# Down projection of a decoder layer: 22 plain K tiles replaced by four plain tiles, seven pairs in seven block products, and four plain tiles

## The chip, the cores and the metric

One Trainium2 chip, one of its cores. The metric is the device time of one execution in microseconds (us), the median of several runs. The engines are TensorE (PE, matrix products; its weight loads are shown apart as PEld), VectorE (DVE), ScalarE (ACT), GpSimd (POOL) and SyncE (SP, which only starts transfers here).

## The reference

One decoder layer on 512 tokens of width 1024: a mixer with two attention groups, then a gated channel mixer of width D_FF = 2816. The part that matters here is the last product and what follows it:

```python
h = rms_norm(x, ffn_pre_norm[l])
f = (jax.nn.silu(h @ w_gate[l]) * (h @ w_up[l])) @ w_down[l]
x = x + rms_norm(f, ffn_post_norm[l])
```

`rms_norm` divides a row by the root of its mean square (plus 1e-6) and multiplies by a gain. `w_down` is 2816 x 1024. All data is float32.

## The kernel before

**Precision.** TensorE multiplies in a reduced format (fp32r). Each float32 operand is split in two tiles: `hi` is the operand copied into fp32r by ScalarE, `lo` is the operand minus `hi`, by VectorE. A product is then three matmuls into one PSUM bank: hi by hi, lo by hi, hi by lo.

**Stages.** The input projection, the two attentions, the output projection and its norm, the up and gate products, and the down projection follow each other. The up and gate products already use block products: `ff_seven` (L952) makes two tiles of D_FF at a time with seven products of blocks, whose sums `ff_prep` (L920) builds; a chain `before[0]` (L904) fixes the order of its matmuls. Its results are the 22 tiles `ffr[f]` (128 of D_FF in the partitions, 512 tokens in the columns), which stay in SBUF in the slots of `sslot` (L162, tiles of 128x512).

**The down projection** (L1026 to L1062, the minus lines of the diff). The result is 512 tokens x 1024 columns: four row tiles of 128 tokens by two halves of 512 columns, `acc[i][c]`, eight PSUM banks that are held through the whole stage. The sum over D_FF goes in 22 K tiles of 128. For each, `down_operands(f)` loads 128x1024 of `w_down` (512 KB; `load_w`, L97, on SyncE's queue) into a rotating raw slot, splits it into `whi` and `wlo` (`split_w`, L111 to L115: ScalarE at L104, VectorE at L114) and splits `ffr[f]` into `ffh` (L104) and `ffl` (L1034). `down` (L1037 to L1042) issues three matmuls for one bank, the two halves of the columns and the four rows in turn: 24 matmuls of 128x512 a K tile, 528 in all. No order is fixed by hand: the scheduler may put them as their operands come.

The first 19 tiles (`NF - LAST`) run tile by tile, all eight banks each. The last three (`LAST = 3`) run row by row: for row tile `i` the three tiles' products for its two banks, and then, while TensorE does the next row, its norm: ScalarE sums the squares from PSUM (`row_rsqrt`, L780), VectorE multiplies the banks by the gain `g_ffn` (L1059), a few one-column steps (`rsqrt_mean`, L122 to L134) make the row's factor `rr`/`rs`, VectorE multiplies by it and adds the residual `x2` (L1061), and SyncE writes the half rows (L1062). `big` (L760) gives tiles of 128x1024 out of named rings, `rope_tile` (L190) tiles of 128x2048, `halves` the two halves of the columns, `wide(tag)` two PSUM banks of a ring, `gain(j)` a loaded gain.

## Time and profile before

| what | value |
|---|---|
| median of 3 runs | 688.05 us (687.72 to 688.37) |
| the profiled execution's own time | 687.77 us |
| its span, first to last instruction | 686.0 us |
| mean granted TensorE clock | 0.98 |
| DMA, mean over the span | 128 GB/s, 87.93 MB |
| instructions | 11052 |

The profile is of one execution. It gives the busy time of each engine and its share of the span, the span in 40 slices, the chain of work that ended last (followed back from the last instruction, at each step to what released it), groups of instructions by source line, and the transfers. A row of a group reads: line, engine, operation, output<-inputs (partitions x elements), number, then busy us and mean ns of one, then the idle time of the engine ahead of them and what ended it. `L1040` is line 1040 of the kernel before. A matmul's recorded length is longer than the distance to the next, since matmuls overlap; so the distance from start to start is what counts. The profiled execution lies 1.8 us above its span (start and end that no engine's record covers) and 0.3 us under the median.

### The profile page before, as it was taken

The page shows a single profiled execution, that of the slowest core. Times are in us where ns is not written, and L with a number is a line of the kernel's source. Part 1 is how long each engine was busy: PE and PEld are TensorE (multiplying, and loading weights), DVE is VectorE, ACT ScalarE, POOL GpSimd, SP SyncE. Part 2 cuts the span into 40 slices and gives each one's busy share as a digit, 9 for nine tenths or more (in the row PEclk, how much of TensorE's full clock was granted, in tenths as well). Part 3 has the DMA queues.
Part 4 walks back from the last instruction along what each step waited for, and adds up shares of the span by engine and source line. Part 5 has one row for each costly group of instructions (what it writes and reads, how often), then busy time and mean ns, then how long its engine had stood idle before and what let it go on. Part 6 is the DMA issues. An engine that isn't in the chain of part 4 may idle for free.

```text
span 686.0 us, 11052 instructions
## 1 busy us (share of the span) xinstructions
PE 651.1 (95%) x4141; PEld 583.5 (85%) x4141; DVE 508.7 (74%) x1015; ACT 367.3 (54%) x775; POOL 78.5 (11%) x86
## 2 busy tenths in 40 slices
PE   9999999999899998797889999999999999999995
PEld 5988787999788787675888999999999988888884
DVE  4878897887999978669898898888888477222227
ACT  7443454568799578435564555655565465212213
POOL 0000000111755323315200000000000000000000
PEclk9999999999999999898799999999999999999998
DMA  8446859671121420252313323332323422332203
GB/s 305 153 139 226 277 198 320 235 246 48 47 94 57 159 93 1 93 210 97 108 64 120 111 93 123 96 120 93 123 94 107 167 96 92 102 112 94 93 0 123
DMA packets 27141, 87.93 MB, mean 128 GB/s; under 512 B 3536, under 2 KB 4432, under 8 KB 26192
## 3 DMA queue, kind: packets, MB, share of 16 engines
q1 hardware_dynamic: 27088, 87.23, 37.8%
q8 instruction: 32, 0.52, 0.3%
q14 instruction: 21, 0.17, 0.1%
HBM read 75.16 MB, written 12.06 MB: 127 GB/s over the span
## 4 chain that ended last, share of the span: by engine, by line
PE 75%; DVE 11%; ACT 6%; DMA 4%; issue 2%; SPq 1%; POOL 0%; DVEq 0%; ACTq 0%
PE gw L913 27%; PE acc L1040 16%; PE fm L290 10%; PE gu L893 5%; PE dv L364 3%; PE mixp L684 3%; ACT p L499 2%; PE tr L509 2%; PE vg L386 2%; DMA wraw<-in_wf 2%; PE sc L493 2%; DVE ptl L514 1%; PE sc L494 1%; DVE p L498 1%; PE avn L637 1%
## 5 line engine op out<-in xcount | busy, mean ns | idle before, releaser
L114 DVE TENSOR_TENSOR wlo<-wraw,whi 128x1024 fp32r<-128x1024 f32 (+2 forms) x58 | 69.9, 1208 | 82.2 <-ACT whi L104 82.0
L104 ACT ACTIVATE whi<-wraw 128x1024 fp32r<-128x1024 f32 (+2 forms) x58 | 60.3, 1045 | 111.2 <-PE acc L1040 66.6
L1040 PE MATMUL acc<-whi,ffl 128*128 128x512 f32 x176 | 68.6, 390 | 0.0
L1040 PE MATMUL acc<-wlo,ffh 128*128 128x512 f32 x176 | 68.1, 390 | 0.0
L1040 PE MATMUL acc<-whi,ffh 128*128 128x512 f32 x176 | 67.2, 390 | 0.4 <-ACT ffh L104 0.4
L518 POOL TENSOR_TENSOR p<-p,l 128x384 f32<-128x384 f32 (+3 forms) x60 | 49.2, 848 | 131.2 <-DVE l L548 58.0
L499 ACT ACTIVATE p<-p,nm 128x128 f32<-128x128 f32 (+1 forms) x96 | 53.2, 556 | 15.3 <-DVE nm L498 14.6
L498 DVE CUSTOM_DVE_ANT_0 p<-sc,mask_b 128x128 f32<-128x128 f32 (+1 forms) x96 | 43.9, 483 | 6.7 <-PE sc L494 6.1
L514 DVE TENSOR_TENSOR ptl<-tr,pth 128x384 fp32r<-128x384 f32 (+1 forms) x60 | 35.6, 595 | 5.8 <-ACT pth L513 5.3
L1040 PEld LDWEIGHTS acc<-whi,ffh 128*128 128x128 f32 x176 | 33.0, 188 | 7.4 <-ACT ffh L104 0.6
L513 ACT ACTIVATE pth<-tr 128x384 fp32r<-128x384 f32 (+1 forms) x60 | 30.8, 517 | 15.3 <-PE tr L509 14.9
L1040 PEld LDWEIGHTS acc<-whi,ffl 128*128 128x128 f32 x176 | 33.1, 188 | 6.9
L1040 PEld LDWEIGHTS acc<-wlo,ffh 128*128 128x128 f32 x176 | 33.1, 188 | 6.8
L509 PE MATMUL tr<-ident,p 128*128 128x128 f32 x200 | 34.2, 290 | 3.9 <-DVE rr L127 2.3
L493 PE MATMUL sc<-kst,qst 128*128 128x128 f32 (+2 forms) x96 | 33.5, 357 | 4.5 <-DVE nm L498 2.9
L290 PE MATMUL fm<-xh,whi 128*128 128x512 f32 x128 | 33.5, 396 | 1.5 <-ACT whi L104 1.5
L509 PEld LDWEIGHTS tr<-ident,p 128*128 128x128 f32 x200 | 25.3, 150 | 8.8 <-DVE ptl L514 3.0
L290 PE MATMUL fm<-xh,wlo 128*128 128x512 f32 x128 | 32.6, 391 | 0.0
L290 PE MATMUL fm<-xl,whi 128*128 128x512 f32 x128 | 32.4, 390 | 0.0
L494 PE MATMUL sc<-kst,qst 128*128 128x128 f32 (+2 forms) x96 | 31.0, 326 | 0.0
L290 PEld LDWEIGHTS fm<-xh,whi 128*128 128x128 f32 x128 | 23.6, 188 | 7.3 <-ACT whi L104 2.1
L290 PEld LDWEIGHTS fm<-xl,whi 128*128 128x128 f32 x128 | 24.0, 188 | 5.0
(292 smaller groups left out, 1717.6 us busy)
## 6 DMA issues: line engine op xcount, KB each, us to landing
wraw<-in_wg SPq DMA_DIRECT2D x22, 512.0 KB, 3.4
wraw<-in_wd SPq DMA_DIRECT2D x22, 512.0 KB, 3.3
wu<-in_wu SPq DMA_DIRECT2D x19, 512.0 KB, 3.3
wraw<-in_wf SPq DMA_DIRECT2D x16, 512.0 KB, 4.8
qk<-rope SPq DMA_DIRECT2D x7, 1024.0 KB, 4.8
kst<-qk SPq DMA_DIRECT2D x24, 256.0 KB, 3.8
qst<-qk SPq DMA_DIRECT2D x16, 256.0 KB, 3.1
wraw<-in_wo SPq DMA_DIRECT2D x8, 512.0 KB, 3.5
```

Source lines behind the costliest of these rows:

```text
L104: act.activation(dst, src, AF.Copy)
L114: (lo_eng or dve).tensor_tensor(lo[:, :w], raw[:, :w], f32(hi[:, :w]), OP.subtract)
L290: pe.matmul(pt, w[:, k * P:(k + 1) * P], xx[k], start=(n == 0), stop=(n == 3 * NK - 1))
L493: pe.matmul(sv, lhs, kk[:, 0, :w], start=True, stop=False)
L494: pe.matmul(sv, lhs, kk[:, 1, :w], start=False, stop=True)
L498: dve.tensor_tensor_reduce(pt, sv, mask_b[:, (NT - 1 - i) * P:], -1.0, BIG, OP.add, OP.min, nm)
L499: act.activation(pt, pt, AF.Exp, bias=nm, scale=-1.0, accum_out=l[:, i:i + 1])
L509: pe.transpose(tr[:, n * P:(n + 1) * P], pts[i][:, j * P:(j + 1) * P], ident)
L514: dve.tensor_tensor(ptl[:, sl], trv, f32(pth[:, sl]), OP.subtract)
L518: pool.tensor_tensor(p, p, l.to_broadcast(list(p.shape)), OP.mult)
L913: m = pe.matmul(pt, ww[:, k * P:(k + 1) * P], hx[k], start=(start and n == 0), stop=(n == 11), skip_group_check=True)
L1040: pe.matmul(acc[i][c], a[:, i * P:(i + 1) * P], w[wi][:, c * SEQ:(c + 1) * SEQ], start=(first and n == 0), stop=(last and n == 2))
```

## The change

It rewrites the down projection and leaves the rest (the order of all engines up to the first matmul of the stage is the same, apart from splits of two weight tiles that came early).

*Plain tiles in front.* K tiles 0 to 3 (`PRE`) are plain, 24 matmuls each, by `d_plain`. The four quarters of the result (256 tokens x 512 columns, two banks each) are C11 in `cc`, C12 in `ca`, C21 in `cb`, C22 in `cd`. Then ScalarE copies C12 and C21 to SBUF (`dps`).

*Seven pairs.* Tiles 4 to 17 are taken two at a time. Of a pair, a11 and a12 are the first and second tile's first 256 tokens, a21 and a22 their other 256; b11 and b12 are the first weight tile's two column halves, b21 and b22 the second's. Instead of eight products of blocks, seven are made, in Winograd's form, each of 2 x 3 matmuls of 128x512. They are split in two passes over all seven pairs. The x pass has three (18 matmuls): a11 b11 into `ca`, -(a21+a22)(b11-b12) into `cb`, a12 b21 into `cc`. Then ScalarE copies `ca` and `cb` to SBUF (L1196) and VectorE adds `cc` and `cd` to these copies (L1199, four steps of 128x512). The y pass has the other four (24 matmuls): two more into `ca` and `cb`, and `cd` and `cc` started anew. At its end `ca` and `cd` are taken into the partial results `u2`, `u3`, `p5` (L1211 to L1215), and POOL's queue starts four accumulating transfers (L1218, 256 KB each) that add the saved C12 and C21 onto `u2` and `u3`.

*Plain tiles behind.* Tiles 18 to 21 are plain; of these the last three run row by row as before. Each bank then holds only a part, so VectorE first adds the saved part (L1237, 128x512, eight steps), the squares are read from SBUF, and the gain product (L1239) and the output (L1241, L1242) follow.

*Operands.* `d_load`, `d_sums` and `d_split` make the operands of a step: the sums of blocks and the low parts on VectorE, the high parts on ScalarE (L1044). The order of the two engines' steps and of all matmuls is written by chains (`queued`, `before[0]`). The operands come in the order four plain, x of pairs 0 to 2, y of pair 0, x of 3 to 6, y of 1 to 6, four plain (`YPOS`, `YN`); `ready` holds them two steps ahead of TensorE (more at the start, `PRELEAD`). Split weights lie in the three ring slots of before and in three more inside `hth` and `htl`, which the gate stage no longer needs. The loads of `w_down` for an x step are one tile and a half, for a y step two; the gain's and the residual's loads stand behind them on SyncE's queue.

The diff:

```diff
...
+HOFF, HSLOTS = 8, 3
+PRE, PAIRS = 4, 7
+AHEAD, PRELEAD = 3, (2, 4, 5, 6, 7, 8, 9, 10, 11)
+YPOS, YN = 3, 1
...
+    L, H = slice(0, SEQ), slice(SEQ, D_MODEL)
+    TL, TH = slice(0, HT), slice(HT, SEQ)
+    queued = {}
...
+    def pair(p):
+        return PRE + 2 * p, PRE + 2 * p + 1
+    raw, ops, nraw = {}, {}, [0]
...
+    def d_load(s):
+        k, p = s
+        t = next_raw()
+        nc.sync.dma_start(t, wd[p if k == "d" else pair(p)[0]])
+        raw[s] = t
+        if k == "x":
+            b21 = f32(sslot("b21"))
+            nc.sync.dma_start(b21, wd[pair(p)[1]][:, L])
+            raw[s] = t, b21
+        elif k == "y":
+            q1 = big("q1")
+            nc.sync.dma_start(q1, wd[pair(p)[1]])
+            raw[s] = t, q1
+    def d_sums(s):
+        k, p = s
+        if k == "d":
+            return
+        a0, a1 = (ffr[f] for f in pair(p))
+        if k == "x":
+            r, b21 = raw[s]
+            s1 = f32(sslot("s1"))[:, :HT]
+            two(r[:, H], r[:, L], r[:, H])
+            two(s1, a0[:, TH], a1[:, TH], OP.add)
+            raw[s] = r, b21, s1
+            return
+        q0, q1 = raw[s]
+        two(q0[:, H], q1[:, H], q0[:, H])
+        two(a0[:, TH], a0[:, TL], a0[:, TH])
+        two(q0[:, L], q0[:, L], q0[:, H], OP.add)
+        two(a0[:, TL], a1[:, TH], a0[:, TH])
+        two(q1[:, L], q1[:, L], q0[:, L])
+        two(a1[:, TL], a1[:, TL], a0[:, TL])
+    def h_slots(j):
+        return [t.rearrange("p k t -> p (k t)")[:, HOFF + j * D_MODEL:HOFF + (j + 1) * D_MODEL] for t in (hth, htl)]
+    def d_split(s):
+        k, p = s
+        if k == "d":
+            if 0 < p < PRE:
+                w = h_slots(p % HSLOTS)
+            else:
+                w = split_slots() if p < NF - 1 else (big("wh", F32R), big("wl", F32R))
+            h = sslot("ffh"), sslot("ffl")
+            parts = [(w, raw.pop(s), 1.0), (h, ffr[p], 1.0)]
+            ops[s] = w, h
+        elif k == "x":
+            r, b21, s1 = raw.pop(s)
+            a0, a1 = (ffr[f] for f in pair(p))
+            w, b, a = split_slots(), (sslot("b21h"), sslot("b21l")), (big("ah", F32R), big("al", F32R))
+            aj = [[t[:, j * HT:(j + 1) * HT] for t in a] for j in range(3)]
+            parts = [(aj[0], a0[:, TL], 1.0), (w, r, 1.0), (aj[2], s1, -1.0), (aj[1], a1[:, TL], 1.0), (b, b21, 1.0)]
+            ops[s] = aj, w, b
+        else:
+            q0, q1 = raw.pop(s)
+            a0, a1 = (ffr[f] for f in pair(p))
+            w0, w1 = (split_slots() if j >= HSLOTS else h_slots(j) for j in ((2 * p) % (HSLOTS + 3), (2 * p + 1) % (HSLOTS + 3)))
+            h0, h1 = ((sslot("ah"), sslot("al")) for _ in range(2))
+            parts = [(h0, a0, 1.0), (w0, q0, 1.0), (h1, a1, 1.0), (w1, q1, 1.0)]
+            ops[s] = w0, w1, h0, h1
+        for (hi, lo), src, sg in parts:
+            q("a", "activation", hi, src, AF.Copy, scale=sg)
+        for (hi, lo), src, sg in parts:
+            if sg > 0:
+                two(lo, src, f32(hi))
+            else:
+                q("d", "scalar_tensor_tensor", lo, src, sg, f32(hi), OP.mult, OP.subtract)
...
+    dps = [big("dp", tag="t21"), big("dp", tag="t21")]
+    pre = [("d", f) for f in range(PRE)]
+    xs, ys = ([(k, p) for p in range(PAIRS)] for k in "xy")
+    last = [("d", f) for f in range(PRE + 2 * PAIRS, NF)]
+    steps, plan = pre + xs + ys + last, pre + xs[:YPOS] + ys[:YN] + xs[YPOS:] + ys[YN:] + last
+    done = {"load": 0, "sums": 0, "split": 0}
...
+    ca, cb, cc, cd = (wide(t, "acc") for t in ("tr", "o", "gu", "o"))
+    result = [[ca, cb], [cc, cd]]
...
+    parts = [f32(rope_tile()) for _ in range(2)]
+    c11, p5, u2, u3 = ([parts[j // 2][:, 2 * (j % 2) + t] for t in range(2)] for j in range(4))
+    for n, s in enumerate(steps):
+        ready(n)
+        k, p = s
+        if n < PRE:
+            d_plain(s, [[cc, ca], [cb, cd]], n == 0, n == PRE - 1, ((0, 1), (1, 0), (1, 1), (0, 0)))
+            if n == PRE - 1:
+                d12, d21 = (halves(t) for t in dps)
+                for d, src in ((d12, ca), (d21, cb)):
+                    for t in range(2):
+                        act.activation(d[t], src[t], AF.Copy)
+        elif k == "x":
+            (a11, a12, s1), w, b21 = ops.pop(s)
+            first, end = p == 0, p == PAIRS - 1
+            d_block(ca, a11, [t[:, L] for t in w], first, end)
+            d_block(cb, s1, [t[:, H] for t in w], first, end)
+            d_block(cc, a12, b21, False, end)
+            if end:
+                for src, o in ((cb, p5), (ca, c11)):
+                    for t in range(2):
+                        act.activation(o[t], src[t], AF.Copy)
+                for src, o in ((cd, p5), (cc, c11)):
+                    for t in range(2):
+                        dve.tensor_tensor(o[t], src[t], o[t], OP.add)
+        elif k == "y":
+            w0, w1, h0, h1 = ops.pop(s)
+            first, end = p == 0, p == PAIRS - 1
+            def mul(pt, h, ts, w, cs, start):
+                d_block(pt, [t[:, ts] for t in h], [t[:, cs] for t in w], start and first, end)
+            mul(ca, h0, TL, w0, L, False)
+            mul(cd, h0, TH, w0, H, True)
+            mul(cb, h1, TL, w1, H, False)
+            mul(cc, h1, TH, w1, L, True)
+            if end:
+                for t in range(2):
+                    act.activation(u2[t], ca[t], AF.Copy)
+                for t in range(2):
+                    dve.tensor_tensor(u3[t], cd[t], u2[t], OP.add)
+                for t in range(2):
+                    dve.tensor_tensor(p5[t], u3[t], p5[t], OP.add)
+                for o, d in ((u2, d12), (u3, d21)):
+                    for t in range(2):
+                        pool.dma_start(o[t], d[t], accum_op=OP.add)
+        elif n < len(steps) - LAST:
+            d_plain(s, result, s == last[0] and ((0, 0), (1, 1)), False, ((0, 1), (1, 0), (1, 1), (0, 0)))
+    part = [[c11[0], u2[0]], [c11[1], u2[1]], [u3[0], p5[0]], [u3[1], p5[1]]]
     g_ffn = gain(2)
-    acc = [wide(t, "acc") for t in ("tr", "o", "gu", "o")]
-
-    def down_operands(f):
-        w = split_w(load_w(wd[f]))
-        hi, lo = sslot("ffh"), sslot("ffl")
-        to_r("a", hi, ffr[f])
-        dve.tensor_tensor(lo, ffr[f], f32(hi), OP.subtract)
-        return w, hi, lo
-
-    def down(i, ops, first, last, c):
-        w, hi, lo = ops
-        for n, (a, wi) in enumerate(((hi, 0), (lo, 0), (hi, 1))):
-            pe.matmul(acc[i][c], a[:, i * P:(i + 1) * P],
-                      w[wi][:, c * SEQ:(c + 1) * SEQ],
-                      start=(first and n == 0), stop=(last and n == 2))
-
-    for f in range(NF - LAST):
-        ops = down_operands(f)
-        for i in range(NT):
-            for c in range(2):
-                down(i, ops, f == 0, False, c)
     for i in range(NT):
         x2[i] = big("x2")
         nc.sync.dma_start(x2[i], x2d[i])
-    ws = [down_operands(f) for f in range(NF - LAST, NF)]
     for i in range(NT):
+        uh = [f32(sslot("uf")) for _ in range(2)]
+        gh = [f32(sslot("ug")) for _ in range(2)]
         for c in range(2):
-            for n, ops in enumerate(ws):
-                down(i, ops, False, n == LAST - 1, c)
-        u, a, x_ = big("uf"), acc[i], halves(x2[i])
-        uh = halves(u)
-        r = row_rsqrt(a, "c", lambda c: dve.tensor_tensor(uh[c], a[c], g_ffn[:, CS[c]], OP.mult))
+            bank = result[i // 2][c][i % 2]
+            for s in last[-LAST:]:
+                w, h = ops[s]
+                d_run(bank, [x[:, i * P:(i + 1) * P] for x in h], [x[:, CS[c]] for x in w],
+                      s == last[0] and c == i // 2, s == last[-1])
+            dve.tensor_tensor(uh[c], bank, part[i][c], OP.add)
+        x_ = halves(x2[i])
+        r = row_rsqrt(uh, "c", lambda c: dve.tensor_tensor(gh[c], uh[c], g_ffn[:, CS[c]], OP.mult))
         for c in range(2):
-            dve.scalar_tensor_tensor(uh[c], uh[c], r, x_[c], OP.mult, OP.add)
-            nc.sync.dma_start(out[i * P:(i + 1) * P, CS[c]], uh[c])
+            dve.scalar_tensor_tensor(gh[c], gh[c], r, x_[c], OP.mult, OP.add)
+            nc.sync.dma_start(out[i * P:(i + 1) * P, CS[c]], gh[c])
 
 
 # ---- launch: one core; inputs laid out for the device ----
```

The places where the written order differs. First TensorE's queue where the down projection begins; `gw` are the last products of the gate stage, `acc` the eight banks by number (6572 to 6579), `whi`/`wlo` and `ffh`/`ffl` the two parts of the weight tile and of the `ffr` tile. Before:

```order
L913 MATMUL gw_6467<-hth_3600,wl_6361 128x256 x4
L1040 MATMUL acc_6572<-whi_6582,ffh_6586 128x512
L1040 MATMUL acc_6573<-whi_6582,ffh_6586 128x512
L1040 MATMUL acc_6574<-whi_6582,ffh_6586 128x512
L1040 MATMUL acc_6575<-whi_6582,ffh_6586 128x512
L1040 MATMUL acc_6576<-whi_6582,ffh_6586 128x512
L1040 MATMUL acc_6578<-whi_6582,ffh_6586 128x512
L1040 MATMUL acc_6579<-whi_6582,ffh_6586 128x512
L1040 MATMUL acc_6572<-whi_6582,ffl_6587 128x512
L1040 MATMUL acc_6572<-wlo_6583,ffh_6586 128x512
```

And now:

```order
L917 MATMUL gw_6467<-hth_3600,wl_6361 128x256 x4
L1136 MATMUL acc_6572<-whi_6588,ffh_6590 128x512
L1136 MATMUL acc_6572<-whi_6588,ffl_6591 128x512
L1136 MATMUL acc_6572<-wlo_6589,ffh_6590 128x512
L1136 MATMUL acc_6573<-whi_6588,ffh_6590 128x512
L1136 MATMUL acc_6573<-whi_6588,ffl_6591 128x512
L1136 MATMUL acc_6573<-wlo_6589,ffh_6590 128x512
```

The first matmul that reads the low part `ffl` stood eighth in the stage and now stands second.

Second, VectorE's queue in the middle of the stage. Before, it holds only low parts, some tiles ahead of TensorE:

```order
L1034 TENSOR_TENSOR ffl_6995<-ff12_5341,ffh_6994 128x512
L114 TENSOR_TENSOR wlo_6719<-wraw_6716,whi_6718 128x1024
L1034 TENSOR_TENSOR ffl_7029<-ff13_5466,ffh_7028 128x512
L1034 TENSOR_TENSOR ffl_7063<-ff14_5591,ffh_7062 128x512
L1034 TENSOR_TENSOR ffl_7097<-ff15_5716,ffh_7096 128x512
```

Now, around the joint between the passes; `al`, `htl` and `wlo` are low parts of pair 1's y step, `dr`, `q1`, `ff10` sums of pair 3's, `rope` the saved copies `p5` and `c11`, `acc` the banks of `cd` (6578, 6579) and `cc` (6576, 6577):

```order
L1044 TENSOR_TENSOR al_7034<-ff6_4591,ah_7033 128x512
L1044 TENSOR_TENSOR htl_3601<-dr_6918,hth_3600 128x1024
L1044 TENSOR_TENSOR al_7036<-ff7_4716,ah_7035 128x512
L1044 TENSOR_TENSOR wlo_7032<-q1_6920,whi_7031 128x1024
L1044 TENSOR_TENSOR dr_7021<-q1_7023,dr_7021 128x512
L1044 TENSOR_TENSOR ff10_5091<-ff10_5091 128x256
L1199 TENSOR_TENSOR rope_6580<-acc_6578,rope_6580 128x512
L1199 TENSOR_TENSOR rope_6580<-acc_6576,rope_6580 128x512
L1199 TENSOR_TENSOR rope_6580<-acc_6577,rope_6580 128x512
L1044 TENSOR_TENSOR dr_7021<-dr_7021 128x512
L1199 TENSOR_TENSOR rope_6580<-acc_6579,rope_6580 128x512
L1044 TENSOR_TENSOR ff10_5091<-ff11_5216,ff10_5091 128x256
```

The four bank additions stand between the sums of the pair after next; the fourth, of `cd`'s second half, stands behind one more sum.

Third, VectorE's queue at the end of the kernel, the last two row tiles; `ss` are sums of squares, `rr`/`rs` the row's factor. Before:

```order
L1059 TENSOR_TENSOR uf_7399<-acc_6578,gain_6570 128x512
L129 SCALAR_TENSOR_TENSOR rr_7369<-rr_7368,rr_7367 128x1
L133 TENSOR_SCALAR rr_7369<-rr_7369 128x1
L134 TENSOR_TENSOR rs_7366<-rr_7368,rr_7369 128x1
L1061 SCALAR_TENSOR_TENSOR uf_7360<-uf_7360,rs_7366,x2_7230 128x512 x2
L787 TENSOR_TENSOR ss_7400<-ss_7400 128x1
L1059 TENSOR_TENSOR uf_7399<-acc_6579,gain_6570 128x512
L127 TENSOR_SCALAR rr_7406<-ss_7400 128x1
L129 SCALAR_TENSOR_TENSOR rr_7408<-rr_7407,rr_7406 128x1
L133 TENSOR_SCALAR rr_7408<-rr_7408 128x1
L134 TENSOR_TENSOR rs_7405<-rr_7407,rr_7408 128x1
L1061 SCALAR_TENSOR_TENSOR uf_7399<-uf_7399,rs_7405,x2_7232 128x512 x2
```

Now:

```order
L1237 TENSOR_TENSOR uf_7562<-acc_6579,rope_6580 128x512
L1239 TENSOR_TENSOR ug_7563<-uf_7561,gain_7419 128x512
L138 TENSOR_TENSOR rs_7546<-rr_7548,rr_7549 128x1
L1239 TENSOR_TENSOR ug_7564<-uf_7562,gain_7419 128x512
L791 TENSOR_TENSOR ss_7585<-ss_7585 128x1
L1241 SCALAR_TENSOR_TENSOR ug_7519<-ug_7519,rs_7546,x2_7425 128x512
L1241 SCALAR_TENSOR_TENSOR ug_7520<-ug_7520,rs_7546,x2_7425 128x512
L131 TENSOR_SCALAR rr_7591<-ss_7585 128x1
L133 SCALAR_TENSOR_TENSOR rr_7593<-rr_7592,rr_7591 128x1
L137 TENSOR_SCALAR rr_7593<-rr_7593 128x1
L1241 SCALAR_TENSOR_TENSOR ug_7563<-ug_7563,rs_7590,x2_7427 128x512
L1241 SCALAR_TENSOR_TENSOR ug_7564<-ug_7564,rs_7590,x2_7427 128x512
```

Each half row now passes through three steps of 128x512 behind its bank (L1237, L1239, L1241) where it passed through two (L1059, L1061).

More of the change, by code (lines that the diff above doesn't have):

```diff
@@ new lines, in two, with next_raw @@
+    def two(o, x, y, op=OP.subtract):
+        q("d", "tensor_tensor", o, x, y, op)
+    def pair(p):
+        return PRE + 2 * p, PRE + 2 * p + 1
+    raw, ops, nraw = {}, {}, [0]
+    def next_raw():
+        nraw[0] += 1
+        if nraw[0] % 5 in (1, 3):
+            return big("dr", tag="ru")
+        return wpool.tile([P, D_MODEL], F32, tag="raw", name="dr", bufs=WB[0])
+    def d_load(s):
[11 more added lines that the diff above has]
+            raw[s] = t, q1
@@ new lines, in d_run, with d_block @@
+    def d_run(pt, a, b, start, stop):
+        m = None
+        for n, (x, y) in enumerate(((a[0], b[0]), (a[1], b[0]), (a[0], b[1]))):
+            with tc.issue_after(before[0]):
+                m = pe.matmul(pt, x, y, start=(start and n == 0), stop=(stop and n == 2), skip_group_check=True)
+        before[0] = getattr(m, "ins", m)
+    def d_block(pt, a, b, start, stop):
+        for t in range(2):
+            d_run(pt[t], [x[:, t * P:(t + 1) * P] for x in a], b, start, stop)
+    dps = [big("dp", tag="t21"), big("dp", tag="t21")]
@@ new lines, in hybrid_block_kernel, with until @@
+    pre = [("d", f) for f in range(PRE)]
[3 more added lines that the diff above has]
+    done = {"load": 0, "sums": 0, "split": 0}
+    todo = {"load": d_load, "sums": d_sums, "split": d_split}
+    def until(what, n):
+        while done[what] < min(n, len(steps)):
+            todo[what](plan[done[what]])
+            done[what] += 1
@@ new lines, in ready, with d_plain @@
+    def ready(n):
+        for j in range(done["split"], 1 + (n + 2 if n >= len(PRELEAD) else PRELEAD[n])):
+            until("load", j + AHEAD)
+            until("sums", j + 2)
+            until("split", j + 1)
+    ca, cb, cc, cd = (wide(t, "acc") for t in ("tr", "o", "gu", "o"))
+    result = [[ca, cb], [cc, cd]]
+    def d_plain(s, banks, first, end, order=((0, 0), (0, 1), (1, 0), (1, 1))):
+        w, h = ops[s]
+        for r, c in order:
+            for t in range(2):
+                i = 2 * r + t
+                d_run(banks[r][c][t], [x[:, i * P:(i + 1) * P] for x in h], [x[:, CS[c]] for x in w],
+                      first and (first is True or (r, c) in first), end)
```

9 lines of the change are left out of this document (added).

## The prediction

> **What bounds the kernel now.** I read the page's first and fourth parts, then the chain of waits in order of time for the last 250 us, then the busy time by stage, and last the timeline around the two ends of the down projection. First lines of the page, and the chain's shares by engine:
>
> ```profile
> span 686.0 us, 11052 instructions
> PE 651.1 (95%) x4141; PEld 583.5 (85%) x4141; DVE 508.7 (74%) x1015; ACT 367.3 (54%) x775; POOL 78.5 (11%) x86
> PE 75%; DVE 11%; ACT 6%; DMA 4%; issue 2%; SPq 1%; POOL 0%; DVEq 0%; ACTq 0%
> ```
>
> TensorE (PE) is busy nearly throughout and carries most of the chain. A busy PE is no proof (matmuls overlap), so the stage itself, on the chain in order of time (start, length, what) and in busy time by stretch:
>
> ```profile
> 557.93 110.51 PE acc L1040 x486
> 681.13 0.75 DVE uf L1061
> ...
> 510.00:530.00 20.00, 20.00 (x172) 20.00 (x170) 17.28 (x25) 11.58 (x21) 0.00 (x0) 1.00 0.34 107
> 558.00:678.00 120.00, 119.94 (x528) 99.04 (x528) 46.45 (x68) 39.26 (x63) 0.00 (x0) 1.00 0.24 78
> ```
>
> The columns are PE, PEld, DVE, ACT, POOL, granted clock, DMA share, GB/s. Through the whole down projection the chain runs through one line, L1040, with no other piece in between; VectorE (DVE) works 46 of 120 us, ScalarE (ACT) 39. The stage is bounded by the number of matmuls. The row above it, a stretch of the gate stage, shows DVE at 17.28 of 20 us with PE still full at clock 1.00: a busy DVE alone does not slow PE.
>
> **The change, part by part.**
>
> *Matmuls removed.* First and last matmul of the stage (start, length):
>
> ```profile
> 557.93 1.90 PE L1040 MATMUL acc<-whi,ffh 128*128 128x512 f32 x7 [0.39 <-ACT ffh L104]
> 559.67 0.40 PE L1040 MATMUL acc<-whi,ffl 128*128 128x512 f32 x1
> ...
> 677.56 0.39 PE L1040 MATMUL acc<-wlo,ffh 128*128 128x512 f32 x1
> ```
>
> From first to last start is 119.63 us over 527 steps: 0.227 us a matmul. A plain K tile has 24 matmuls (5.45 us). A pair took 48; seven block products of 2 x 3 matmuls take 42. Seven pairs drop 42 of 528, all of the same 128x512 form: 42 x 0.227 = **-9.53 us**, if PE never waits. The rest of this part asks where it would.
>
> *PE's written order at the start.*
>
> ```profile
> 557.26 0.61 ACT L104 ACTIVATE ffh<-ff 128x512 fp32r<-128x512 f32 x1
> 557.91 0.69 DVE L1034 TENSOR_TENSOR ffl<-ff,ffh 128x512 fp32r<-128x512 f32 x1
> ```
>
> Before, seven hi products come first and cover DVE's low part. Now the second matmul (due 557.93 + 0.23 = 558.16) needs ffl, finished at 558.60 and seen some 0.05 later: **+0.49 us**. The gate stage in front is unchanged on PE, so the start stays.
>
> *DVE's new work.* What matters is the start-to-start step, not the length of one:
>
> ```profile
> 510.96 0.43 DVE L978 TENSOR_TENSOR ff<-cx 128x256 f32<-128x256 f32 x1 [0.15 <-ACT cx L977]
> 511.31 0.68 DVE L947 TENSOR_TENSOR t<-wraw,t 128x512 f32<-128x512 f32 x1
> ...
> 514.60 1.22 DVE L935 TENSOR_TENSOR wlo<-t,whi 128x1024 fp32r<-128x1024 f32 x1
> 515.73 0.69 DVE L935 TENSOR_TENSOR t4l<-t,t4h 128x512 fp32r<-128x512 f32 x1
> 516.34 0.69 DVE L939 TENSOR_TENSOR t<-wu,t 128x512 f32<-128x512 f32 x1
> 516.94 0.68 DVE L946 TENSOR_TENSOR wu<-wu 128x512 f32<-128x512 f32 x1
> ```
>
> A step is 0.35 us for 256 columns, 1.13 for 1024, 0.60 for 512; the 256-wide scalar_tensor_tensor has no row, I take 0.37 (0.35 to 0.43, the neighbour's full length). An x step has sums of 512 and 256 (0.95) and low parts of 3 x 256, 1024 and 512 (2.80): 3.75 us, against 18 matmuls, 4.09. A y step has sums of 3 x 512 and 3 x 256 (2.85) and low parts of 2 x 512 and 2 x 1024 (3.46): 6.31 us, against 24 matmuls, 5.45. So DVE gains 0.34 on PE in each x and loses 0.86 in each y. Seven of both: DVE 70.4, PE 66.8. The cover is the four plain tiles in front: PE needs 21.8 us for them, DVE 4 x 1.73 = 6.9 and about 1.0 for the rest of the last gate tile. DVE's lead of 13.9 pays the 3.6 and the four bank additions behind the x pass (4 x 0.60 = 2.4). DVE also waits, by my walk along its queue: 0.3 us while ACT loads its table (1.28 us) ahead of the third tile's high part,
>
> ```profile
> 559.67 1.28 ACT L981 ACT_TABLE_LOAD   x1
> ```
>
> and 0.5 at the first y's low part, whose high part goes into a slot that PE frees only with the last plain matmul (557.93 + 0.49 + 21.8 = 580.2). DVE is then through with the last y at 557.9 + 6.9 + 1.0 + 70.4 + 2.4 + 0.8 = 639.4. PE begins that y at 580.2 + 7 x 4.09 + 6 x 5.45 + 0.7 (below) = 642.2 and needs its last operand half a step later, at 644.9: 5 us to spare. The weight slots (three) let DVE stand at most some three steps ahead in the x pass; there x3's slot comes free when PE ends x0 (584.3) and its operands are done by 588.1, due 592.5.
>
> *ACT* gets 128x256, 512 and 1024 copies:
>
> ```profile
> L104 ACT ACTIVATE whi<-wraw 128x1024 fp32r<-128x1024 f32 x22 | 23.3, 1060 | 67.3 <-PE acc L1040 66.6 <-PE gw L913 0.7
> L104 ACT ACTIVATE ffh<-ff 128x512 fp32r<-128x512 f32 x22 | 12.6, 620 | 4.5 <-DVE ffl L1034 4.4
> L963 ACT ACTIVATE cx<-gw 128x256 f32<-128x256 f32 x6 | 2.2, 368 | 1.4 <-PE gw L913 1.4
> ```
>
> An x costs 3 x 0.37 + 1.06 + 0.62 = 2.8 us, a y 2 x 1.06 + 2 x 0.62 = 3.4: under PE in both, so nothing.
>
> *The joint between the passes.* PE's first y block writes ca, then cd. Bank cd is started anew and must have been read by DVE's additions (L1199), of which the fourth stands behind one y sum. DVE reaches the first at 557.9 plus 49.4 us of queued steps (four plain tiles, seven x, three y sums, two y low parts, two sums of the fourth) plus the 0.8 waited: 608.2; the fourth ends three 0.60 steps and a 0.60 sum later plus 0.69, near 611.3 to 611.6. PE wants that half-bank at 580.2 + 28.6 + 9 x 0.227 = 610.9. **+0.4 to 0.7 us**; I take 0.7. Each us that DVE is late here costs one.
>
> *Loads.* The pairs' weights are read twice in part; the stage moved 78 GB/s with a landing of 3.3 us,
>
> ```profile
> wraw<-in_wd SPq DMA_DIRECT2D x22, 512.0 KB, 3.3
> x<-x2d SPq DMA_DIRECT2D x4, 512.0 KB, 5.5
> ```
>
> and its loads now stand in one queue behind slots that PE or DVE free. The tightest by my walk has 2.6 us beyond 3.3 (the second x's half tile), so 5.5, four loads at once, still hides: nothing.
>
> *The end.*
>
> ```profile
> 680.24 0.14 DVE L127 TENSOR_SCALAR rr<-ss 128x1 f32<-128x1 f32 x1
> 681.13 1.41 DVE L1061 SCALAR_TENSOR_TENSOR uf<-uf,rs,x 128x512 f32<-128x512 f32 x2
> ```
>
> From the last matmul's end (677.95) to DVE's last (682.54) were 4.59 us. Now DVE adds a saved part to each bank first (8 more steps of 0.60), and a row of tokens costs it 4.3 us against PE's 18 matmuls, 4.09. Behind the last matmul it has one addition, two gain products, two one-column steps, row 2's two outputs, the 0.89 from rr to the outputs and row 3's two: 0.60 + 1.20 + 0.14 + 1.33 + 0.89 + 1.41 = 5.57, begun 0.05 to 0.4 after the matmul: **+1.0 to +1.4**, taken as 1.2.
>
> *Four accumulating DMAs on POOL's queue.* Before has none there. They are issued near 647 and first needed (row by row) at 657.2, 661.3, 663.4 and 667.5. Of 256 KB there are rows from 2.1 to 7.1 us:
>
> ```profile
> out<-uf SPq DMA_DIRECT2D x8, 256.0 KB, 2.1
> cst<-in_consts SPq DMA_DIRECT2D x1, 256.0 KB, 7.1
> ```
>
> If they go one after the other, the fourth is the tight one and they hide up to 20.5 / 4 = 5.1 us each. They add onto SBUF within the core as `out` moves from it, in a quiet stretch, so I take a price near 2.1 to 3.8 (hidden); 7.1 stays for the range: 28.4 against 20.5, less 2 us until row 3's own last addition, +5.9. The Trainium skill ("DMA: Bandwidth & Descriptors", "Anatomy of one DMA — SWDGE (gpsimd) path") fits about 2.0 us plus bytes / 436e3 per us for this path, by which each would take some 2.6 us (an estimate) and the sum would stay as it is.
>
> **Sum.** -9.53 + 0.49 + 0.7 + 1.2 = -7.1 us. The profiled execution took 687.77 us (span 686.0), so 680.6; the median of the three runs is 688.05, 0.28 above it: **680.9**. Without the joint's wait and with the smaller end it is 680.0.
>
> **The rivals.**
>
> *DVE becomes the bound.* If DVE's instructions could not overlap their ends, a step would be the length (0.69, 0.43, 1.22): 0.6 more per x, 0.87 per y, 0.7 in front and 0.4 at the joint, together 11.4 us. DVE would then end the last y near 651 where PE needs it at 644.9: 6 us of waits, 686.9. For it: DVE is the engine with the least slack here, at 70.4 of 66.8. Against it: 516.34 to 516.94 is 0.60 with a length of 0.69, again and again. This is the rule of the Trainium skill, "VectorE: DVE Perf Modes", "The DRAIN you can't avoid", that the next operation does not start until the pipe is empty; the rows here disagree with it. A part of it can come all the same (waits between the two engines that fall in unlucky order), so the times between 683.5 and 687 belong to it.
>
> *The accumulating DMAs end last.* Place: row 3's addition behind POOL's fourth transfer. In series at d us each, past 5.6 the end moves by 4 d - 22.5; it decides against the change from d = 7.4. At 9.2 (7.1 and a second trip of 2.1, since the destination is read too) the time is 680.9 + 14.3 = 695.2. For it: no row of this kind in the trace. Against: ten us of slack for the first.
>
> *It hides better than I think*: no waits at the joint and the start, an end that grows by 0.5: 679.3 or less.
>
> *It doesn't do what it says*: the built order has 486 matmuls in the stage, so this keeps only the remainder.
>
> **How the numbers follow.** Two runs of this kernel differ by 0.1%, so about 0.2%, 1.4 us, can be told from no change. Forecast (679.3 to 683.5) 0.72; DVE-bound (683.5 to 687.3) 0.15, a third of it within 0.2%; DMAs 0.06; better than 679.3 0.05; remainder 0.02. Faster: 0.72 + 0.05 + 0.10 = 0.87; same 0.05 + 0.02 = 0.07; slower 0.06. The range 679.0 to 685.5 leaves out the DMA case and the far half of the DVE case, and holds the 7.1 us price only at its near side.
>
> **What would show it.** The stage with 486 matmuls of 0.227 us in about 111.5 us; waits of PE only at its second matmul (0.5) and at the first y for L1199 (0.7); DVE near 75% busy in the pairs with the last y's low parts some 5 us ahead of PE; last matmul to DVE's end near 5.8 us; POOL's DMAs landing before 660. Wrong: waits of PE for DVE in the y pass adding up to over 3 us, or DVE waiting for POOL in the last rows.

## The result, and the profile after

| | before | changed |
|---|---|---|
| median | 688.21 us (687.72 to 688.38, 4 runs) | 681.82 us (680.75 to 683.93, 4 runs) |
| ratio of the times | 1 | 0.9912, 95% interval 0.9888 to 0.9936 |
| the profiled execution's own time | 687.77 us | 681.76 us |
| its span | 686.0 us | 680.0 us |

The forecast was 680.9 us with a range of 679.0 to 685.5. The time fell by 6.4 us in the medians and by 6.0 in the profiled executions, where the sum had 7.1. So direction and most of the size came as forecast, and 1.1 us are missing. The page of the changed kernel, first part and shares of the chain by engine:

```profile
span 680.0 us, 11179 instructions
PE 644.9 (95%) x4099; PEld 576.7 (85%) x4099; DVE 562.7 (83%) x1122; ACT 389.6 (57%) x820; POOL 82.2 (12%) x90
PE 79%; DVE 9%; ACT 5%; DMA 4%; issue 2%; POOL 1%; SPq 0%; DVEq 0%; ACTq 0%
```

PE has 4099 matmuls where it had 4141: the 42 are gone. DVE has 54 us more work, and its share of the chain is smaller than before. The chain in order of time through the stage (start, length, what):

```profile
557.74 0.70 DVE ffl L1044
558.44 0.04 issue
558.49 108.05 PE acc L1136 x467
666.54 0.02 issue
666.56 0.69 DVE uf L1237
```

From the second matmul on, 467 run without another engine's piece between them; the chain leaves PE at row 2's second bank because the last rows' norm on DVE ends later than PE. The whole stage in busy time (PE, PEld, DVE, ACT, POOL, granted clock, DMA share, GB/s):

```profile
558.00:671.00 113.00, 112.47 (x486) 90.93 (x485) 101.17 (x174) 63.08 (x109) 3.68 (x4) 1.00 0.48 159
```

DVE is busy 101 of 113 us at full clock. In the pairs alone it is 65.27 of 68.00 us, 96%:

```profile
580.40:648.40 68.00, 68.00 (x296) 55.14 (x295) 65.27 (x104) 40.50 (x61) 0.58 (x1) 1.00 0.48 170
```

Which waits PE had for others in and around the stage (in total, times, longest):

```profile
PE acc L1136 <- ACT ffh L1044: 0.4, 1, 0.4
PE acc L1136 <- DVE ffl L1044: 0.2, 1, 0.2
```

The first was there before too. No wait for DVE of any size stands in the two passes. First, second, a matmul of the joint and the last on PE, with their starts:

```profile
557.76 0.50 PE L1136 MATMUL acc<-whi,ffh 128*128 128x512 f32 x1 [0.39 <-ACT ffh L1044]
558.49 0.50 PE L1136 MATMUL acc<-whi,ffl 128*128 128x512 f32 x1 [0.22 <-DVE ffl L1044]
...
611.61 0.40 PE L1136 MATMUL acc<-htl,ah 128*128 128x512 f32 x1
611.92 0.50 PE L1136 MATMUL acc<-hth,ah 128*128 128x512 f32 x1
...
670.30 0.40 PE L1136 MATMUL acc<-wl,ffh 128*128 128x512 f32 x1
```

The second stands 0.73 behind the first, where 0.23 is the usual step: 0.50 lost. At the joint (cd's second half) the step is 0.31: 0.08 lost. From the first start to the last one's end the stage takes 670.70 - 557.76 = 112.94 us; before it took 120.02. DVE's last addition and the outputs of the last two rows, with which it ends:

```profile
671.09 0.68 DVE L1237 TENSOR_TENSOR uf<-acc,rope 128x512 f32<-128x512 f32 x1
...
673.03 1.41 DVE L1241 SCALAR_TENSOR_TENSOR ug<-ug,rs,x 128x512 f32<-128x512 f32 x2
...
675.24 1.41 DVE L1241 SCALAR_TENSOR_TENSOR ug<-ug,rs,x 128x512 f32<-128x512 f32 x2
```

From the last matmul's end to DVE's end (676.65) are 5.95 us, 4.59 before.

What is missing is in none of these places. If 42 matmuls at 0.227 us had gone and 0.58 of waits come, the stage would be 120.02 - 9.53 + 0.58 = 111.07 us. It is 112.94: apart from four long ones, the steps between the 486 matmuls that are left take 0.2304 us on average, 0.0036 more than before. The time by stretches shows it. A stretch of the x pass, and one of the y pass with weights in the ring, counting PE's line L1136 alone (PE, PEld, clock, DMA share, GB/s):

```profile
586.00:606.00 20.00, 20.00 (x87) 16.14 (x86) 1.00 0.58 196
620.00:626.00 6.00, 6.00 (x28) 4.95 (x28) 1.00 0.24 87
```

The same stretches of the kernel before, its line L1040:

```profile
586.00:606.00 20.00, 20.00 (x90) 16.59 (x89) 1.00 0.31 94
620.00:626.00 6.00, 6.00 (x28) 4.99 (x27) 1.00 0.25 87
```

In 20 us of the x pass PE makes 87 matmuls where it made 90, at a full clock and with no wait. Over many triples of matmuls the steps are 0.2267 before, throughout; after, 0.2333 in the x pass, 0.229 where the weights lie inside `hth` and `htl`, and 0.2315 in the last rows. The step changes exactly where the operands' homes change, and in stretches of 2 us it is the same whether DMA moves 4 or 390 GB/s beside it.

### The profile page after: what moved, and what is told of

It is laid out like the page before. It is cut to its first block, busy times and chain, and to the rows that moved or that the text cites. A ratio compares the mean times of both kernels' runs of the same rounds, so it can differ in the third digit from the quotient of the medians.

```text
span 680.0 us, 11179 instructions
## 1 busy us (share of the span) xinstructions
PE 644.9 (95%) x4099; PEld 576.7 (85%) x4099; DVE 562.7 (83%) x1122; ACT 389.6 (57%) x820; POOL 82.2 (12%) x90
## 4 chain that ended last, share of the span: by engine, by line
PE 79%; DVE 9%; ACT 5%; DMA 4%; issue 2%; POOL 1%; SPq 0%; DVEq 0%; ACTq 0%
PE gw L917 28%; PE acc L1136 16%; PE fm L294 10%; PE gu L897 5%; PE dv L368 3%; PE mixp L688 3%; PE tr L513 3%; PE avn L641 2%; PE vg L390 2%; DMA wraw<-in_wf 2%; PE sc L497 2%; ACT p L503 2%; PE sc L498 1%; DVE p L502 1%; DMA gain<-in_grow 1%
## 5 line engine op out<-in xcount | busy, mean ns | idle before, releaser
L108 ACT ACTIVATE whi<-wraw 128x1024 fp32r<-128x1024 f32 (+2 forms) x36 | 37.1, 1037 | 43.4 <-PE fm L294 17.8
L118 DVE TENSOR_TENSOR wlo<-wraw,whi 128x1024 fp32r<-128x1024 f32 (+2 forms) x36 | 42.9, 1197 | 18.6 <-ACT whi L108 18.6
L1218 POOL DMA_DIRECT2D rope<-dp x4 | 3.7, 1129 | 318.7 <-DVE rope L1213 318.7
L294 PEld LDWEIGHTS fm<-xh,wlo 128*128 128x128 f32 x128 | 23.8, 188 | 4.8
L497 PEld LDWEIGHTS sc<-kst,qst 128*128 128x128 f32 x96 | 18.6, 194 | 7.6 <-DVE nm L502 6.1
L1044 ACT ACTIVATE ah<-ff 128x256 fp32r<-128x256 f32 (+1 forms) x28 | 14.3, 512 | 14.5 <-DVE ff L1044 11.1
L917 PE MATMUL gw<-rope,whi 128*128 128x256 f32 x160 | 21.9, 279 | 0.0
L972 DVE TENSOR_TENSOR cy<-gw,cy 128x512 f32<-128x512 f32 x19 | 13.0, 684 | 10.7 <-PE gw L917 10.7
```

Source lines behind the costliest of these rows:

```text
L108: act.activation(dst, src, AF.Copy)
L118: (lo_eng or dve).tensor_tensor(lo[:, :w], raw[:, :w], f32(hi[:, :w]), OP.subtract)
L294: pe.matmul(pt, w[:, k * P:(k + 1) * P], xx[k], start=(n == 0), stop=(n == 3 * NK - 1))
L497: pe.matmul(sv, lhs, kk[:, 0, :w], start=True, stop=False)
L917: m = pe.matmul(pt, ww[:, k * P:(k + 1) * P], hx[k], start=(start and n == 0), stop=(n == 11), skip_group_check=True)
```

## The experiments

The theories on the slower step: **A**, where each operand starts (the x step's parts of `ffr` and the last weights lie in 128x1024 tiles, which start 32 bytes past a multiple of 64); **B**, the traffic of DVE, ACT and the transfers, which is about twice what it was. The starts come from the addresses that the built program gives its tiles; the profile does not show them, and an edit moves them by the bytes that it names. Both were sharpened on the way. The others test terms of the forecast.

**e1: all operands of the stage at 64 past a multiple of 128.**

```diff
-HOFF, HSLOTS = 8, 3
+HOFF, HSLOTS, XOFF = 24, 3, 24
-                w = split_slots() if p < NF - 1 else (big("wh", F32R), big("wl", F32R))
+                w = split_slots() if p < NF - 1 else h_slots(2)
-            aj = [[t[:, j * HT:(j + 1) * HT] for t in a] for j in range(3)]
+            aj = [[t[:, XOFF + j * HT:XOFF + (j + 1) * HT] for t in a] for j in range(3)]
```

> The changed kernel with the same instructions in the same order; only the operands that TensorE reads in the down projection are moved so that all start at 64 bytes past a multiple of 128, as they did before the change (the x step's high and low parts of ffr by 96 bytes, the slots inside hth and htl by 64, the last tile's weights into such a slot). Theory A (where an operand starts sets the pitch of the matmuls): the pitch falls from 0.2333 us in the x pass, 0.229 with hth and htl, and 0.2315 in the last rows to 0.2267 throughout; last matmul about 1.9 us earlier; the time falls by 1.5 to 1.9 us, to 680. Theory B (VectorE's, ScalarE's and the transfers' traffic slows TensorE's reads): the traffic is the same, so pitch and time stay within 0.3 us.

683.16 us, ratio 0.9921 (0.9901 to 0.9942): no gain. The step in the x pass stays at 0.2333, and with the slots inside `hth` and `htl` it is worse, 0.2333 in place of 0.229. Theory A in this form is refuted. B isn't shown by it either, since a step got longer under the same traffic.

**e2: only the x step's parts moved, to a multiple of 128** (the last line of e1's edit alone, with XOFF = 8).

> The changed kernel with only the x step's high and low parts of ffr moved by 32 bytes, to a multiple of 128 (before: 32 past a multiple of 64). Theory A: the x pass leaves 0.2333 for 0.2267 (if only the place within 64 bytes counts) or 0.229 (if the place within 128 counts, as hth and htl with 0 against 64 suggest); the y pass and the last rows stay as they were. Theory B: the x pass stays at 0.2333.

683.65 us (one run); the x pass stays at 0.2333. A again gave a wrong number, and B the right one.

**e3 and e4: the padding moved, so that `hth`, `htl` and the 128x1024 tiles lie 32 bytes lower, in the kernel before and in the changed one.**

```diff
-    pad = ctx.enter_context(tc.tile_pool(name="pad", bufs=1, side="left"))
-    pad.tile([P, 8], F32, name="pad")
     sum_alloc()
+    A.tile([P, 8], F32, name="pad")
```

> The kernel before the change, its instructions and order untouched, with 32 bytes of padding moved from one side of the memory to the other so that hth, htl, the rope tiles and the 128x1024 tiles, which lay at 32 past a multiple of 64, lie at multiples of 64. These are operands of the gate stage only, not of the down projection. Theory A: the gate stage's 128x256 matmuls, 0.120 us apart where both operands lie at 32 and 0.115 to 0.1175 where one does, come to 0.1133, 1596 x 0.004 = 5 to 6 us off the time; the down projection stays at 0.2267. Theory B: no change.

> The changed kernel with the same move of the 32 bytes of padding (slots inside hth and htl from their start). Theory A: the gain of the gate stage as in the kernel before, 5 to 6 us, and the 1.5 to 1.9 us of the down projection: 674 to 675. The change by itself is then worth 8.5 to 9 us against the kernel before with the same move. Theory B: no change from 681.8. Against both: VectorE may not keep up with a faster gate stage (it was busy 17.28 of 20 us there), which would give waits of PE for DVE in the gate stage and take part of the gain.

e3: 690.99 us, ratio 1.0041 (1.0026 to 1.0055), slower where 5 to 6 us of gain were expected. e4: 683.01, 0.9928 (0.9908 to 0.9948). But e4's down projection has the step of before in the x pass too. Its line is L1135:

```profile
586.00:606.00 20.00, 20.00 (x90) 16.57 (x89) 1.00 0.56 177
```

90 matmuls in 20 us under a DMA share of 0.56: B is refuted, since DVE, ACT and the transfers do here what they did in the changed kernel. The stage takes 111.45 us. What was won there was lost in the gate stage, whose 128x256 matmuls became slower in both kernels: from its first to its last group 191.0 us in place of 188.0. The gate line of e3, and behind it of the kernel before:

```profile
380.00:550.00 170.00, 170.00 (x1419) 170.00 (x1418) 1.00 0.33 108
```

```profile
380.00:550.00 170.00, 170.00 (x1442) 170.00 (x1441) 1.00 0.34 112
```

What e1 and e4 differ in are the starts of the two operands of a matmul against each other. In the kernel before and in e4 both operands of every down matmul start at the same place within 512 bytes. In the changed kernel the x step's are 32 bytes apart, those with `hth` and `htl` 64, in e1 128, in e2's x pass 64 the other way round. That is theory **A2**; its rival **E** is that the homes of what DVE, ACT and the transfers touch decide.

**e5: in the changed kernel both operands of every down matmul at the same place within 512 bytes**, nothing else moved. As e1, with 120 in place of 24.

> The changed kernel, same instructions and order; only the x step's parts of ffr, the slots inside hth and htl and the last tile's weights are moved (by 480, 448 bytes, and into such a slot), so that in the whole down projection the two operands of every matmul start at the same place within 512 bytes. Theory A2 (what counts is the difference of the two operands' starts within 512 bytes, none being best for 128x512: e1, whose starts all lay at 64 past 128 but 128 or 384 apart, kept 0.2333, and e4, where none was apart, had 0.2267): 0.2267 throughout, the last matmul 1.6 to 1.9 us earlier after the first, the time 679.5 to 680.5; the gate stage as before. Theory A (the place within 64 or 128 of each operand): as e1, 0.233. Theory E (in e4 it was the start of what VectorE, ScalarE and the transfers touch, or the move of the gate stage's operands, and not TensorE's own operands): 0.229 to 0.2333 as in the changed kernel, since these stay where they are.

680.94 us, ratio 0.9889 (0.9864 to 0.9914). The scatter of the runs does not separate this time from the changed kernel's; the trace does. The same stretches as above, L1136:

```profile
586.00:606.00 20.00, 20.00 (x90) 16.57 (x89) 1.00 0.62 206
620.00:626.00 6.00, 6.00 (x28) 4.99 (x27) 1.00 0.28 88
```

0.2267 throughout, and the stage takes 111.48 us in place of 112.94; the gate stage takes 187.95 in both. A2 gave the number and E did not. The stage gained 1.46 and not 1.73, what 481 steps of 0.0036 make, because PE now reaches the joint earlier and waits there:

```profile
610.85 0.39 PE L1136 MATMUL acc<-htl,ah 128*128 128x512 f32 x1
611.43 0.50 PE L1136 MATMUL acc<-hth,ah 128*128 128x512 f32 x1 [0.19 <-DVE rope L1199]
```

0.58 in place of 0.23: a wait of 0.35, by DVE's fourth bank addition.

**e6: the reverse, the kernel before with operands 32 bytes apart.** The padding stands ahead of the 128x512 tiles and no longer behind them.

> The kernel before the change, same instructions and order, with the 32 bytes of padding moved so that the tiles of 128x512 (ffh and ffl among them) lie 32 bytes further and the weight slots stay. All 528 matmuls of the down projection then have operands that start 480 apart within 512 bytes. Theory A2: their pitch goes from 0.2267 to 0.2333, 528 x 0.0066 = 3.5 us, and with the gate stage's t4 products (228 matmuls, now none apart, 0.115 to 0.120: 1 us) and the input projection 4 to 7 us slower than 688.3. Theory E: 0.2267, no change of time.

695.03 us, ratio 1.0087 (1.0061 to 1.0113). Line L1040:

```profile
586.00:606.00 20.00, 20.00 (x87) 16.14 (x86) 1.00 0.30 93
```

87 again, at the kernel before's light traffic: all 528 steps at 0.2333, the stage 123.46 us in place of 120.02, +3.44 where 3.5 was expected. The rest lies ahead of the stage, which begins 4.4 us later (the input projection uses the same tiles: its steps went from 0.2276 to 0.2334, and it ends 1.3 us later; the gate stage, where 228 more matmuls start none apart, takes 0.8 us longer; the other 2.3 us in between are not accounted for). With e5, this shows A2 in both directions. It is the place of the operands against each other, not the place itself: in the output projection (L696) e6 moves both operands of every matmul by the 32 bytes, and its steps stay, 0.2286 before and 0.2283 in e6.

**e7: one more DVE step in each y step.**

```diff
         two(q0[:, H], q1[:, H], q0[:, H])
+        two(q0[:, L], q0[:, L], q0[:, H])
```

> The changed kernel with one more 128x512 step on VectorE in each y step's sums (it subtracts one sum from another once more, so the products are of other numbers). My forecast's reading: VectorE's tight place is the joint, where four y sums stand ahead of the fourth bank addition: 4 x 0.60 = 2.4 us later there, so PE waits 2.3 to 2.5 us in place of 0.08; the end of the y pass has 7 us to spare and takes 7 x 0.60 = 4.2 without a wait: 684. Rival (VectorE has slack at the joint too, the additions being waited for only by chance): below 683, wait under 1 us. Rival (VectorE bounds the whole y pass): 4.2 us and more, waits of PE for VectorE in the y pass.

684.05 us (one run), but the waits at the joint are 0.44 and 0.07, and not 2.4. That the time is the 684 expected is luck: the stage is only 0.49 us longer than in the changed kernel, and it begins 1.82 us later, behind stages that the edit does not touch. Its DVE queue there (the additions are L1200 here):

```profile
603.82 0.68 DVE L1044 TENSOR_TENSOR dr<-q,dr 128x512 f32<-128x512 f32 x1
604.53 0.69 DVE L1044 TENSOR_TENSOR dr<-dr 128x512 f32<-128x512 f32 x1
...
610.83 0.68 DVE L1044 TENSOR_TENSOR dr<-q,dr 128x512 f32<-128x512 f32 x1
611.44 1.87 DVE L1200 TENSOR_TENSOR rope<-acc,rope 128x512 f32<-128x512 f32 x3
613.48 0.69 DVE L1200 TENSOR_TENSOR rope<-acc,rope 128x512 f32<-128x512 f32 x1 [0.17 <-ACT rope L1197]
614.09 0.68 DVE L1044 TENSOR_TENSOR dr<-dr 128x512 f32<-128x512 f32 x1
```

The additions are not in the written chain; the scheduler put the fourth two steps further ahead than in the changed kernel and `cd`'s two halves behind `cc`'s, and DVE's wait for ACT at the first y's low part shrank from 0.93 to 0.17 us. So the fourth ended only 0.5 us later after the first matmul (54.6 against 54.1), and PE was held about as much longer: 0.44 for the third addition (`cd`'s first half, ended at 613.31) and 0.07 for the fourth, against 0.08. That a late addition costs PE its lateness agrees; my 2.4 had taken the additions' place as fixed, so e7 does not show what the joint costs with DVE later and the order kept. In the y pass PE had no wait for DVE, as the forecast's reading says: the 4.2 us went into the slack. (The first two rows are a sum and the added step, which needs it: 0.71 from start to start and not 0.60.)

**e8: additions on DVE in place of the accumulating transfers.**

```diff
-                        pool.dma_start(o[t], d[t], accum_op=OP.add)
+                        dve.tensor_tensor(o[t], o[t], d[t], OP.add)
```

> The changed kernel with the four accumulating transfers on POOL's queue replaced by four additions of 128x512 on VectorE at the same place. My forecast's reading (the transfers were hidden, in 6 us of idle VectorE): VectorE's idle time ahead of the first row falls by 2.4 us, nothing moves at the end, the time is the changed kernel's within its scatter. Rival (the transfers hold row 0's or row 1's addition, or slow what reads beside them): last matmul to VectorE's end falls from 5.95 us by over 0.3 us.

682.47 us (one run). DVE's idle time ahead of the first row falls from 6.23 to 3.83 us, the 2.4 expected; the stage is 112.94 and the end 5.94, both as in the changed kernel. In the changed kernel the transfers were thus hidden:

```profile
rope<-dp POOLq DMA_DIRECT2D x4, 256.0 KB, 5.0
```

5.0 us from issue to landing at the median; the four overlap, from the first issue at 647.8 to the last landing at 656.1.

**e9 and e10: a layout that suits the down projection and, as I thought, the gate stage**, in the changed kernel and in the one before.

```diff
     g_post, g_pre = gain(0), gain(1)
+    A.tile([P, 120], F32, name="pad1")
...
+    A.tile([P, 8], F32, name="pad2")
     hth = A.tile([P, NK, SEQ], F32R, name="hth")
-    junk = {t: A.tile([P, SEQ], BF16, name="junk" + t, bufs=1) for t in "ab"}
-    junk["c"] = junk["a"]
+    junk = dict.fromkeys("abc", A.tile([P, SEQ], BF16, name="junk", bufs=1))
```

> The changed kernel, same instructions and order apart from one scratch tile shared by two uses, with padding so that the down projection's operands all start none apart within 512 bytes and, of the gate stage's 1596 matmuls of 128x256, only 228 are none apart (672 in the changed kernel) and the others 32 apart. Theory A2: the down projection as in e5 (111.5 us from first matmul to the last's end); the gate stage, where none apart cost 0.120 and 32 apart 0.111 to 0.1175, gains (672 - 228) x 0.004 = 1.8 us; together 3.3 us below the changed kernel. Rival (the gate stage's pitch has another cause, as its two values of 0.115 and 0.1175 hint): no gain there, 1.5 us in all.

> The kernel before the change with the same padding. Theory A2: down projection unchanged (0.2267 already), gate stage as in e9, 1.8 us faster than before. The difference from e9 is then the change by itself: 120.0 - 111.5 in the stage, 1.4 lost at the end: 7.1 us, the sum of my forecast. Rival: no gain in the gate stage.

e9: 684.79 us, ratio 0.9952 (0.9932 to 0.9971). e10: 692.06, 1.0065 (1.0044 to 1.0086). Both are slower than without the layout, and for a reason outside the question: the norms between the output projection and the gate stage share one scratch tile now, and the gate stage starts 3.1 to 3.7 us later. I take the sharing for the cause, since DVE waits 3.3 us there for ACT's squares in e10 and 1.4 in the kernel before, but I did not undo it alone. The gate stage itself gains nothing (188.0 us in both). None apart is the dearer step there too (0.1195 us for the 228 that are left, 0.1199 in the kernel before), but the matmuls 32 apart, 0.1167 before, take 0.1178 in this layout, and that cancels the gain; why they do is open. The down projection is as expected, 111.44 and 119.98 us. And the two differ by nothing but the change: 692.06 - 684.79 = 7.3 us between the medians, 6.9 between the profiled runs, where the forecast's sum was 7.1.

**e11: e9 with the first tile's high products ahead and the gain products on POOL.**

```diff
-            d_plain(s, [[cc, ca], [cb, cd]], n == 0, n == PRE - 1, ((0, 1), (1, 0), (1, 1), (0, 0)))
+            if n == 0:
+                (wh_, wl_), (fh_, fl_) = ops[s]
...
+                for g in (((fh_, wh_),), ((fl_, wh_), (fh_, wl_))):
...
-        r = row_rsqrt(uh, "c", lambda c: dve.tensor_tensor(gh[c], uh[c], g_ffn[:, CS[c]], OP.mult))
+        r = row_rsqrt(uh, "c", lambda c: pool.tensor_tensor(gh[c], uh[c], g_ffn[:, CS[c]], OP.mult))
```

> e9 with two more edits: the first plain tile's eight products of high parts first (so that the second matmul does not wait for VectorE's low part), and the norm's gain products of the last rows on POOL in place of VectorE. From the terms as measured: the wait of 0.5 us at the second matmul goes; of the 5.95 us from the last matmul to VectorE's end about 1.4 go, since VectorE's 8 gain steps of 0.60 leave its queue and a gain step on POOL (128x384: 0.85 us) lies beside ScalarE's squares. 1.9 us below e9. Rival for the second (POOL's steps are slower, or slow VectorE's beside them): the last stretch stays at 5.5 or more.

685.99 us, ratio 0.9976 (0.9958 to 0.9993): 1.2 us above e9 where 1.9 below was expected. The wait of 0.5 at the second matmul is gone:

```profile
561.09 2.11 PE L1193 MATMUL acc<-whi,ffh 128*128 128x512 f32 x8 [0.41 <-ACT ffh L1045]
```

but the stage is only 0.14 shorter, 111.30: the wait at the joint grew from 0.35 to 0.69, since DVE is no earlier there. The end grew from 6.00 to 7.70 us. POOL's groups, and DVE's at that place (busy, mean ns of one):

```profile
L1255 POOL TENSOR_TENSOR ug<-uf,gain 128x512 f32<-128x512 f32 x8 | 10.2, 1284 | 12.3 <-DVE uf L1253 9.1 <-DVE rr L131 2.3 <-DVE rs L138 0.9
...
L1257 DVE SCALAR_TENSOR_TENSOR ug<-ug,rs,x 128x512 f32<-128x512 f32 x8 | 6.6, 871 | 0.4
...
L138 DVE TENSOR_TENSOR rs<-rr 128x1 f32<-128x1 f32 x4 | 2.4, 593 | 0.1
```

In the changed kernel the one-column step L138 took 158 ns and L1241, the same operation as L1257, 748. One-column steps of 1.03 and 1.19 us stand here beside POOL's, and they end when POOL's step does, here at 673.97 and 673.96:

```profile
672.70 1.26 POOL L1255 TENSOR_TENSOR ug<-uf,gain 128x512 f32<-128x512 f32 x1 [2.28 <-DVE rr L131]
672.78 1.19 DVE L133 SCALAR_TENSOR_TENSOR rr<-rr 128x1 f32<-128x1 f32 x1
```

So DVE waits inside its instructions while POOL works. This is the rule of the Trainium skill, "SBUF — State Buffer", "SBUF: two separate sides", that VectorE with two SBUF inputs and GpSimd take a shared port pair in turn, each for a whole instruction; the durations here agree.

**e12: the changed kernel once more, beside e9 to e11.**

> The changed kernel once more, beside the three others on one chip, to have its time and the scatter of its runs next to theirs. Theory A2: the pitches of the down projection come out as in the first profile (0.2333 in the x pass, 0.229 with the slots inside hth and htl), since they hang on addresses and not on the run; a stage of 112.9 us. Rival (they belong to a run's state): other values.

682.08 us (681.64 to 684.57, 6 runs), ratio 0.9922 (0.99 to 0.9944). The steps are those of the first profile (0.2333 in the x pass, 0.2292 with `hth` and `htl`, the stage 112.96 us), so they do not hang on the run. None of the versions is shown to beat the changed kernel; e5 has the shortest trace, 1.1 us of span below it, with an interval of its time that overlaps.

## Why the prediction was right, point by point

- **Matmuls removed, -9.53.** The count was right (486), and "if PE never waits" held. The step that was mis-sized is the price of those that stay: 0.227 was taken for all 128x512 matmuls, and 481 steps came out at 0.2304 (the other four hold the waits). Operands in new homes, whose starts are 32 or 64 bytes apart within 512, cost 1.73 us (e5, e6). This is more than the 1.1 us that are missing: the joint, 0.6 below its forecast, gave a part back, and that was not foreseen.
- **Start, +0.49.** 0.50 measured. In e11 its removal was worth only 0.14, since the joint is next.
- **DVE's queue.** The steps are the start-to-start ones: in the y pass 0.60 and 1.14 for rows that last 0.68 and 1.22. DVE reached the first bank addition at 608.55 (608.2 forecast) and ended the last y's low part at 638.95 (639.4); PE needed it at 645.6, half a step into a y that began at 642.87, so 6.7 us were to spare where 5 were forecast. The rival that the full lengths count is refuted. The section of the Trainium skill on which it leaned, "The DRAIN you can't avoid" in "VectorE: DVE Perf Modes", says too that a next operation that is not held starts earlier; the 0.60 agrees with that, and a step that needs the one just ahead stood 0.71 behind it (e7). One sign did not come, "DVE near 75% busy in the pairs": it was busy 96%, and the prediction's own sum, 70.4 us of DVE beside 66.8 of PE, already left no room for 75%.
- **Joint, +0.7.** 0.08 measured. DVE was where the forecast had it (the fourth addition ended at 611.86; 611.3 to 611.6 forecast); PE was later, at 611.84 and not 610.9, because of its longer step. With the step of before (e5, e9) the wait is 0.35 in both, half of what I took and just under its lower end.
- **End, +1.0 to +1.4.** 1.36.
- **Accumulating transfers, 0.** Hidden (e8), though each took 5.0 us and not 2.1 to 3.8 (nor the 2.6 estimated from the Trainium skill, "DMA: Bandwidth & Descriptors", "Anatomy of one DMA — SWDGE (gpsimd) path"), and they ran together and not in series. The rival with its 7.4 us was far from deciding.
- **Loads.** None reached PE or DVE. ACT stood idle for 3.6 us ahead of the first of the last plain tiles' high parts (at 637.73). That tile's load had landed at 618.08, so it was not the load; probably it was the weight slot, from which PE's last matmul with the old high part started at 636.97. PE needs the tile 10 us later.

The sum again, with what the traces show, against 687.77: 42 matmuls less -9.53, the longer step +1.87 (what the stage holds beyond 111.07: 1.73 by the 481 steps, 0.11 by one step of 0.34 behind the joint, the rest rounding), waits +0.58, end +1.36, the stage's start earlier by 0.17, and 0.12 less behind DVE's end: -6.01, as measured.

What stays open is why the gate stage's 128x256 matmuls 32 bytes apart took 0.1167 us in the kernel before and 0.1178 in e9 and e10. Also open is why the runs of every version here scatter by 1.7 to 5.4 us. The first three of the kernel before lay within 0.65, and the prediction took its 0.1% from them; 18 later runs of the same kernel spread over 4.4 us.

## What to carry to other kernels

When a change gives operands new homes, don't take the old step of a matmul for granted: look at where its two operands start in memory, against each other, and check the step by stretches in the first trace. A saving ahead of a joint where another engine sets the pace is given back there in part (0.27 of 1.73 us in e5), so price it by the joint's slack. And an engine that is nearly always busy, as DVE here at 101 of 113 us, need not cost anything if its lead is built up in front and its start-to-start steps are used for the sum.
